# Block inversion on GpSimd, and the second memory scores inside the third query projection

## The chip, the core and the metric

The kernel runs on one core of one Trainium2 chip. The core has five engines with a queue of instructions each: TensorE (PE; matmuls, with PEld for its weight loads), VectorE (DVE), ScalarE (ACT), GpSimd (POOL) and SyncE (SP, which here only issues transfers). [...] Tiles live in SBUF (on-chip memory) and, for matmul results, in PSUM, whose banks GpSimd does not use in this kernel. Transfers between the device's memory and SBUF run on 16 engines of their own; those issued from SP are called hardware_dynamic in the profile, those from POOL software_dynamic. The metric is the device time of one execution in microseconds, as the median of several runs.

## The reference

Two layers over 512 tokens of width 1024. The change lies in the first, a gated DeltaNet layer with six heads of 128 and a cross-attention with four heads of 64 into 256 memory tokens. Cut to what matters:

```python
proj = h @ w_in                        # q, k, v (6 heads x 128 each), z, gates, mem_q (256)
qkv = silu(causal_depthwise_conv(proj[..., :o1], conv_w))
q, k = l2_normalize(q), l2_normalize(k)
# per chunk and head:
lower = where(strict, (k * beta) @ k.T * decay, 0)
sol = triangular_solve(lower, [v * beta, k * beta * exp(gc)], unit_diagonal=True)
u, w = sol
intra = (q @ k.T) * decay
# scan over the chunks of a head:
v_new = u - w @ state
o = (q * exp(gc)) @ state + intra @ v_new
state = state * g_last + k_g.T @ v_new
# beside it, per memory head:
p = softmax(mem_q @ mem_k.T / 8);  mem_o = p @ mem_v
# then: output projection, residual, SwiGLU; the second layer is sliding-window attention
```

## The kernel before

**Layout.** Activations are held transposed, 128 features by 512 tokens, as eight pairs (`self.h`) of a rounded high part and the remainder (`h`, `l` in the profile). The kernel uses chunks of 128 tokens, so NC = 4 chunks and NH = 24 head-chunks. A projection (`projected`, line 208) takes a weight tile of 128 by 1024 (`wraw`, two buffers, loaded from SP at line 177), splits it into `whi` on ScalarE (line 138) and `wlo` on VectorE (line 151), and runs eight steps of three matmuls (`mm3`, line 196; the profile shows them at line 144) into a bank of the tag `pj`. It is a generator: a caller can take a few steps, put other work in between, and go on.

**Banks.** In this stage PSUM has three banks `pj`, two `g`, three `sc` (line 255). Key products, query products and transposes go to `g`; memory scores take two of `g`, then two of `sc`.

**Order.** Instructions go to each engine's queue in an order that a planner fixes beforehand, from the program's order and modelled costs; a queue runs in that order. `nosync(ins, after)` (line 114) puts one instruction behind another in that order, without a semaphore wait. `self.last` is the last matmul of a step, `self.loaded` the last weight load issued from SP.

**The stage (`gdn`, line 552).** Keys are projected, normalized and turned; for each head-chunk the strict lower triangle goes to `N` (line 629). Its 32 by 32 diagonal blocks, four per head-chunk and 96 in all, are written to memory (`basein`, line 634). Then come the z projections with their Silu, and in between the first memory queries. At line 658 ScalarE's table is set to the exponentials and the first memory scores are made (`scores`, line 909: eight matmuls of a 64-row half each, maxima on VectorE, exponentials on ScalarE). After the second memory queries stands `base_inverse` (line 772):

- It loads the 96 blocks with one block on each partition (`L`, shown as `big`), clears `X` with ones on its diagonal, and inverts all blocks at once by 31 steps of two `tensor_tensor` on VectorE (lines 789 and 791; shown at line 151 as `btmp` and `big`), from 96x31 up to 96x256 elements and down again.
- ScalarE makes a turned copy (line 793). SP stores both (`basex`, `basext`, line 797) and loads them back as block diagonals: `X64` with four transfers (line 804, shown as `X`), `Tt` with four (line 809). VectorE clears both first; all clearings are held behind the last `N` (`known`).

**Queries and memory.** Two groups of three heads follow (line 698). `memory(m, first, late)` (line 667) makes the scores of memory half m (only for m = 1, with the table set to the exponentials again), projects the group's first query, takes two steps of the second, then the query products left in `late`, then `weigh` (line 959: scale the probabilities, transpose them into `g`, evict to `pf` on ScalarE, multiply by the values into `sc`), and the other six steps. The convolution (`conv_tile`, line 542) is one ScalarE copy and three VectorE instructions per head on `qv` (five buffers). Then the table goes to Silu and each head's `query` (line 683) runs: four products `g<-qv,kn`, `DT` and `gcr` multiplied on VectorE, a square `sq` (one buffer) on ScalarE, which SP stores. Of the first group, heads 0 and 1 run at once, behind the third projection; head 2 is put into `late` and runs in the second group's second projection. So the order on TensorE is: query projections 0, 1 (with the first weighing), 2, query products 0 and 1, second scores, projections 3, 4 (with query product 2 and the second weighing), 5.

**After it.** `solve` (line 812) extends the inverse from 32 to 64 and to 128 by products on TensorE. Its first products `sc<-X,N` need X64, the next ones Tt. Value projections and the scan follow. In the later stages GpSimd issues transfers that add to their target and does four multiplications near the end; in this stage it has nothing to do.

Of the kernel before, what the change touches and what calls it, by code (L numbers as in the profile page):

```python
# [18 lines left out]
P = 128  # L19
# [3 lines left out]
H = 6  # L23
# [61 lines left out]
class Builder:  # L85
# [466 lines left out]
    def gdn(self, gp):  # L552
# [67 lines left out]
        for h in range(H):  # L620
# [7 lines left out]
            for c in range(NC):  # L628
                known = self.stt(N[h][:, c, :], ps[:, chunk(c)], br[h][:, c:c + 1], d[:, c, :], ALU.mult, ALU.mult)
# [31 lines left out]
        X, every_t = self.base_inverse(gp, base_in, known)  # L661
        Tt = [every_t[:, h * NC:(h + 1) * NC, :] for h in range(H)]
# [4 lines left out]
        def memory(m, first, late):  # L667

            if m:
                self.use(LN_EXP)  # L670
                scores.append(self.scores(gp, qm[m], self.memK[m], False))
            ps = self.normed(first)
# [25 lines left out]
        for h0 in (0, 3):  # L698
            ps = memory(h0 // 3, h0, late)
            ts = [self.conv_tile(h0 + n, self.t(gp, [P, T], F32, "qv", 5), ps[n] if n < 2 else None) for n in range(3)]  # L700
            behind = self.last
            self.use(SILU_SIN)
            for h, t in zip(range(h0, h0 + 3), ts):
                self.fn(t, t, AF.Silu)
                if h == 2:
                    late.append((h, t))
                else:
                    query(h, t, behind)
# [63 lines left out]
    def base_inverse(self, gp, base_in, after):  # L772
# [10 lines left out]
        clear = lambda out, value: self.nosync(nc.vector.memset(out, value).ins, after)  # L783
        clear(Xf, 0.0)
        clear(Xf[:, ::BASE + 1], 1.0)
        for j in range(BASE - 1):
            r, w = BASE - 1 - j, j + 1
            tmp = self.t(gp, [n, 256], F32, "btmp", 2)[:, :r * w].rearrange("p (i m) -> p i m", m=w)
            self.tt(nc.vector, tmp, L[:, j, j + 1:].unsqueeze(2).to_broadcast([n, r, w]),
                    X[:, j, :w].unsqueeze(1).to_broadcast([n, r, w]), ALU.mult)  # L790
            self.tt(nc.vector, X[:, j + 1:, :w], X[:, j + 1:, :w], tmp, ALU.subtract)
        Xt = big(0)
        self.copy(Xt, X.rearrange("p i m -> p m i"))
        outs = []
        for nm, src in (("basex", X), ("basext", Xt)):
            d = self.t(self.dpool, [NH, NB, BASE * BASE], F32, nm)
            nc.sync.dma_start(d.rearrange("n b e -> (n b) e"), src.rearrange("p a b -> p (a b)"))
            outs.append(d)
        X64 = self.t(gp, [P, NH, 2 * BASE], F32, "X64")
        clear(X64, 0.0)  # L800
        for b in range(NB):
            s = slice(b * BASE, (b + 1) * BASE)
            o = b % 2 * BASE
            nc.sync.dma_start(X64[s, :, o:o + BASE], outs[0][:, b, :].rearrange("n (i m) -> i n m", m=BASE))
        Tt = self.t(gp, [P, NH, P], F32, "Tt")
        clear(Tt, 0.0)
        for b in range(NB):
            s = slice(b * BASE, (b + 1) * BASE)
            nc.sync.dma_start(Tt[s, :, s], outs[1][:, b, :].rearrange("n (m i) -> m n i", i=BASE))
# [99 lines left out]
    def scores(self, pool, q, kk, win, sinks=None):  # L909
# [8 lines left out]
        for n0 in range(0, NC, 2):  # L918
# [5 lines left out]
            for n in (n0, n0 + 1):  # L924
                ks = slice((n - 1) * P if n else 0, (n + 1) * P) if win else slice(0, ML)
                c0 = P if win and n == 0 else 0
                for b in range(2):
                    self.ahead = self.mm(ps[b][:, n - n0, c0:], q[half[b], n * P:(n + 1) * P], kk[half[b], ks])
                    if self.valued is not None:

                        self.nosync(self.ahead, self.valued)
                        self.valued = None
            for b in range(2):
# [805 lines left out]
```

## Time and profile before

| | us |
|---|---|
| three runs | 1116.19, 1117.37, 1118.53 (median 1117.37) |
| the profiled execution | 1116.54 |
| its span, first to last instruction | 1114.8 |
| TensorE busy | 1103.3 |
| VectorE busy | 936.2 |
| ScalarE busy | 696.7 |
| GpSimd busy | 105.9 |

The span is 1.7 us shorter than the profiled execution's time; the granted clock is 0.999. The page gives for each engine busy time, share of the span and instructions. Matmuls are pipelined, and one counts as busy from its start to a modelled end, so a full row of TensorE does not mean that it never waited; its weight loads (PEld) show waits better. "a <- b" in a group of waits says that a stood still until b ended. In a timeline a row gives start, length, engine, line, output and inputs, with the wait before it in brackets. The slices of the page show GpSimd nearly empty up to about 300 us of the span:

```
POOL 0000000000011111111110000000111111111101
```

### The profile page before, as it was taken

Reading aid. Unit: us, or ns where it says so; the run is one execution under the profiler, and the core shown is the slowest. Engines: PE = TensorE matmul, PEld = TensorE weight load, DVE = VectorE, ACT = ScalarE, POOL = GpSimd, SP = SyncE. Lnnn points to the kernel's source line nnn. Section 1 sums busy time; section 2 is a strip of 40 time slices with the busy share of each in tenths; the row PEclk is TensorE's granted clock in tenths of the full one; section 3 lists DMA queues with packets and bytes.
Section 4 is the critical chain, followed back from the end, with each engine's and each line's share of the span. In section 5 each row is a group of like instructions: output and inputs, shape, how many; then the busy total and the mean of one; then the engine's idle time right before and its main releaser. Section 6 shows DMA issues by size and latency. Waiting matters only on the chain.

```text
span 1114.8 us, 21268 instructions
## 1 busy us (share of the span) xinstructions
PE 1103.3 (99%) x7957; PEld 1000.3 (90%) x7957; DVE 936.2 (84%) x1886; ACT 696.7 (62%) x1466; POOL 105.9 (9%) x129
## 2 busy tenths in 40 slices
PE   9999999999999999999999999999999999999997
PEld 8888778877889999999998777788899999999996
DVE  7675977667899999999997877839999899998964
ACT  7588674466556656665565564866766566655644
POOL 0000000000011111111110000000111111111101
PEclk9999999999999999999999999999999999999999
DMA  8344352234467787778853321114678877777632
GB/s 319 99 153 145 107 142 87 86 100 137 148 165 196 186 193 190 178 184 197 199 138 99 118 72 39 57 58 142 161 174 196 198 180 182 191 192 198 154 85 90
DMA packets 81146, 165.36 MB, mean 148 GB/s; under 512 B 18588, under 2 KB 20148, under 8 KB 81044
## 3 DMA queue, kind: packets, MB, share of 16 engines
q1 hardware_dynamic: 64436, 133.87, 38.0%
q0 software_dynamic: 16320, 29.89, 16.4%
q8 instruction: 62, 1.02, 0.4%
q14 instruction: 40, 0.33, 0.1%
q10 hardware_dynamic: 288, 0.26, 0.1%
HBM read 156.98 MB, written 7.01 MB: 147 GB/s over the span
## 4 chain that ended last, share of the span: by engine, by line
PE 78%; DVE 17%; ACT 2%; issue 2%; DMA 0%; DVEq 0%; ACTq 0%; SPq 0%
PE g L144 43%; PE pj L144 23%; PE sc L144 6%; DVE wlo L151 5%; PE qk L144 2%; DVE fu L151 2%; PE pt L148 1%; DVE wraw L151 1%; PE pt L144 1%; DVE l L154 1%; DVE x L151 1%; DVE T L151 1%; DVE l L151 1%; DVE sqa L151 1%; DVE fg L151 1%
## 5 line engine op out<-in xcount | busy, mean ns | idle before, releaser
L138 ACT ACTIVATE whi<-wraw 128x512 fp32r<-128x512 f32 (+2 forms) x357 | 251.8, 711 | 156.5 <-PE g L144 68.6
L151 DVE TENSOR_TENSOR wlo<-wraw,whi 128x512 fp32r<-128x512 f32 (+2 forms) x357 | 279.3, 788 | 34.8 <-ACT whi L138 28.8
L144 PE MATMUL g<-T,whi 128*128 128x256 f32 x1280 | 228.8, 279 | 0.7 <-ACT fs L138 0.6
L144 PE MATMUL g<-l,whi 128*128 128x256 f32 (+1 forms) x780 | 222.9, 286 | 0.5 <-DVE l L151 0.5
L144 PE MATMUL g<-h,whi 128*128 128x256 f32 (+1 forms) x780 | 222.6, 285 | 0.0
L144 PE MATMUL g<-h,wlo 128*128 128x256 f32 (+1 forms) x780 | 222.5, 285 | 0.0
L144 PEld LDWEIGHTS g<-T,whi 128*128 128x128 f32 x1280 | 195.1, 188 | 1.6 <-ACT fs L138 1.1
L144 PE MATMUL pj<-h,whi 128*128 128x512 f32 (+1 forms) x460 | 182.1, 399 | 0.0
L144 PE MATMUL pj<-l,whi 128*128 128x512 f32 (+1 forms) x460 | 180.3, 392 | 0.6 <-DVE l L154 0.6
L144 PE MATMUL pj<-h,wlo 128*128 128x512 f32 (+1 forms) x460 | 179.8, 392 | 0.0
L144 PE MATMUL g<-T,wlo 128*128 128x256 f32 x640 | 178.5, 279 | 0.0
L144 PEld LDWEIGHTS g<-l,whi 128*128 128x128 f32 x780 | 146.6, 188 | 3.0 <-DVE l L151 1.1
L144 PEld LDWEIGHTS g<-h,whi 128*128 128x128 f32 x780 | 146.6, 188 | 1.9
L144 PEld LDWEIGHTS g<-h,wlo 128*128 128x128 f32 x780 | 146.6, 188 | 1.7
L144 PEld LDWEIGHTS g<-T,wlo 128*128 128x128 f32 x640 | 120.3, 188 | 0.0
L144 PEld LDWEIGHTS pj<-h,whi 128*128 128x128 f32 x460 | 86.3, 188 | 20.7 <-issue 4.1
L144 PEld LDWEIGHTS pj<-l,whi 128*128 128x128 f32 x460 | 86.6, 188 | 18.2 <-DVE l L154 1.7
L144 PEld LDWEIGHTS pj<-h,wlo 128*128 128x128 f32 x460 | 86.5, 188 | 17.9 <-issue 0.9
L138 ACT ACTIVATE whi<-ws 128x512 fp32r<-128x512 f32 x112 | 70.3, 627 | 44.5 <-PE g L144 42.0
L151 DVE TENSOR_TENSOR wlo<-ws,whi 128x512 fp32r<-128x512 f32 x112 | 76.5, 683 | 3.6 <-ACT whi L138 3.6
L1386 POOL DMA_DIRECT2D ws<-in_wgu x40 | 35.1, 878 | 447.7 <-DVE sqa L151 203.9
L138 ACT ACTIVATE fs<-g 128x256 f32<-128x256 f32 x168 | 61.5, 366 | 1.3 <-PE g L144 0.9
(398 smaller groups left out, 1926.5 us busy)
## 6 DMA issues: line engine op xcount, KB each, us to landing
wraw<-in_wgu SPq DMA_DIRECT2D x48, 512.0 KB
ws<-in_wgu SPq DMA_DIRECT2D x80, 256.0 KB
ws<-in_wgu POOLq DMA_DIRECT2D x80, 256.0 KB, 5.3
wraw<-in_win SPq DMA_DIRECT2D x26, 512.0 KB
wraw<-in_wgu SPq DMA_DIRECT2D x40, 256.0 KB
wraw<-in_wout SPq DMA_DIRECT2D x16, 512.0 KB
ws<-in_wdn SPq DMA_DIRECT2D x32, 256.0 KB
ws<-in_wdn POOLq DMA_DIRECT2D x32, 256.0 KB, 5.5
```

What stands on the lines that cost most here:

```text
L138: self.copied = self.nc.scalar.activation(out, in_, AF.Copy, **kw).ins
L144: return self.nc.tensor.matmul(out, lhsT, rhs, start=start, stop=stop, skip_group_check=more).ins
L148: return self.nc.tensor.transpose(out, in_, self.ident[:k, :k]).ins
L151: return eng.tensor_tensor(out=out, in0=a, in1=b, op=op).ins
L154: return self.nc.vector.scalar_tensor_tensor(out=out, in0=in0, scalar=scalar, in1=in1, op0=op0, op1=op1).ins
L1386: nc.gpsimd.dma_start(s1, a22, accum_op=ALU.add)
```

## The change

Four things are done.

1. The inversion's 62 `tensor_tensor`, the turned copy, the clearings of `X`, `X64` and `Tt` go to GpSimd. The two stores are issued from GpSimd's queue instead of SP's. The clearings are no longer held behind `N`.
2. The loads of `X64` and `Tt` stay on SP but are split off into `base_blocks`, called in the second group after `memory`, and held behind the last weight load issued there, that of the fifth query projection.
3. The second memory scores are made two steps into the third query projection, by a new argument `after` of `scores`; the table is not set to the exponentials again.
4. All three heads of the first group are put into `late`. The query products 0 and 1 run three steps into the fourth projection, product 2 two steps into the fifth as before.

```diff
--- before.py
+++ after.py
@@ -626,7 +626,7 @@
             for c in range(NC):
                 self.mm(ps[:, chunk(c)], kn[h][:, chunk(c)], kn[h][:, chunk(c)])
             for c in range(NC):
-                known = self.stt(N[h][:, c, :], ps[:, chunk(c)], br[h][:, c:c + 1], d[:, c, :], ALU.mult, ALU.mult)
+                self.stt(N[h][:, c, :], ps[:, chunk(c)], br[h][:, c:c + 1], d[:, c, :], ALU.mult, ALU.mult)
             if h % 2:
                 for b in range(NB):
                     s = slice(b * BASE, (b + 1) * BASE)
@@ -658,18 +658,19 @@
         self.use(LN_EXP)
         scores = [self.scores(gp, qm[0], self.memK[0], False)]
         memory_queries(1)
-        X, every_t = self.base_inverse(gp, base_in, known)
-        Tt = [every_t[:, h * NC:(h + 1) * NC, :] for h in range(H)]
+        outs = self.base_inverse(gp, base_in)
         for i in range(NH):
             h, c = divmod(i, NC)
             self.copy(kg[h][:, c, :], kg[h][:, c, :], scale=f[:, 2, i:i + 1])
 
         def memory(m, first, late):
 
+            steps = self.projected(a["win"][first], self.h)
             if m:
-                self.use(LN_EXP)
-                scores.append(self.scores(gp, qm[m], self.memK[m], False))
-            ps = self.normed(first)
+                nxt = [next(steps) for _ in range(3)]
+                while len(late) > 1:
+                    query(*late.pop(0), self.last)
+            ps = list(steps)[-1]
             steps = self.projected(a["win"][first + 1], self.h)
             nxt = [next(steps) for _ in range(2)]
             self.ahead = self.last
@@ -697,12 +698,22 @@
         late = []
         for h0 in (0, 3):
             ps = memory(h0 // 3, h0, late)
-            ts = [self.conv_tile(h0 + n, self.t(gp, [P, T], F32, "qv", 5), ps[n] if n < 2 else None) for n in range(3)]
+            if h0:
+                X, every_t = self.base_blocks(outs, self.loaded)
+                Tt = [every_t[:, h * NC:(h + 1) * NC, :] for h in range(H)]
+            conv = lambda n, ps: self.conv_tile(h0 + n, self.t(gp, [P, T], F32, "qv", 5), ps)
+            ts = [conv(n, ps[n]) for n in range(2)]
+            steps = self.projected(a["win"][h0 + 2], self.h)
+            if not h0:
+                for _ in range(2):
+                    next(steps)
+                scores.append(self.scores(gp, qm[1], self.memK[1], False, self.last))
+            ts.append(conv(2, list(steps)[-1]))
             behind = self.last
             self.use(SILU_SIN)
             for h, t in zip(range(h0, h0 + 3), ts):
                 self.fn(t, t, AF.Silu)
-                if h == 2:
+                if h < 3:
                     late.append((h, t))
                 else:
                     query(h, t, behind)
@@ -769,7 +780,7 @@
         finish(second)
         return mix + mq
 
-    def base_inverse(self, gp, base_in, after):
+    def base_inverse(self, gp, base_in):
 
         nc = self.nc
         n = NH * NB
@@ -780,33 +791,37 @@
         nc.sync.dma_start(L.rearrange("p a b -> p (a b)"), base_in.rearrange("n b e -> (n b) e"))
         X = big(1)
         Xf = X.rearrange("p a b -> p (a b)")
-        clear = lambda out, value: self.nosync(nc.vector.memset(out, value).ins, after)
-        clear(Xf, 0.0)
-        clear(Xf[:, ::BASE + 1], 1.0)
+        self.blocks = [self.t(gp, [P, NH, n], F32, nm) for nm, n in (("X64", 2 * BASE), ("Tt", P))]
+        for out, value in ((Xf, 0.0), (Xf[:, ::BASE + 1], 1.0), *((x, 0.0) for x in self.blocks)):
+            nc.gpsimd.memset(out, value)
         for j in range(BASE - 1):
             r, w = BASE - 1 - j, j + 1
             tmp = self.t(gp, [n, 256], F32, "btmp", 2)[:, :r * w].rearrange("p (i m) -> p i m", m=w)
-            self.tt(nc.vector, tmp, L[:, j, j + 1:].unsqueeze(2).to_broadcast([n, r, w]),
+            self.tt(nc.gpsimd, tmp, L[:, j, j + 1:].unsqueeze(2).to_broadcast([n, r, w]),
                     X[:, j, :w].unsqueeze(1).to_broadcast([n, r, w]), ALU.mult)
-            self.tt(nc.vector, X[:, j + 1:, :w], X[:, j + 1:, :w], tmp, ALU.subtract)
+            self.tt(nc.gpsimd, X[:, j + 1:, :w], X[:, j + 1:, :w], tmp, ALU.subtract)
         Xt = big(0)
-        self.copy(Xt, X.rearrange("p i m -> p m i"))
+        nc.gpsimd.tensor_copy(Xt, X.rearrange("p i m -> p m i"))
         outs = []
         for nm, src in (("basex", X), ("basext", Xt)):
             d = self.t(self.dpool, [NH, NB, BASE * BASE], F32, nm)
-            nc.sync.dma_start(d.rearrange("n b e -> (n b) e"), src.rearrange("p a b -> p (a b)"))
+            nc.gpsimd.dma_start(d.rearrange("n b e -> (n b) e"), src.rearrange("p a b -> p (a b)"))
             outs.append(d)
-        X64 = self.t(gp, [P, NH, 2 * BASE], F32, "X64")
-        clear(X64, 0.0)
+        return outs
+
+    def base_blocks(self, outs, after):
+
+        nc = self.nc
+        X64, Tt = self.blocks
         for b in range(NB):
             s = slice(b * BASE, (b + 1) * BASE)
             o = b % 2 * BASE
-            nc.sync.dma_start(X64[s, :, o:o + BASE], outs[0][:, b, :].rearrange("n (i m) -> i n m", m=BASE))
-        Tt = self.t(gp, [P, NH, P], F32, "Tt")
-        clear(Tt, 0.0)
+            self.nosync(nc.sync.dma_start(
+                X64[s, :, o:o + BASE], outs[0][:, b, :].rearrange("n (i m) -> i n m", m=BASE)).ins, after)
         for b in range(NB):
             s = slice(b * BASE, (b + 1) * BASE)
-            nc.sync.dma_start(Tt[s, :, s], outs[1][:, b, :].rearrange("n (m i) -> m n i", i=BASE))
+            self.nosync(nc.sync.dma_start(
+                Tt[s, :, s], outs[1][:, b, :].rearrange("n (m i) -> m n i", i=BASE)).ins, after)
         return X64, Tt
 
     def solve(self, gp, N, X64, Tt):
@@ -906,7 +921,7 @@
         return new
 
 
-    def scores(self, pool, q, kk, win, sinks=None):
+    def scores(self, pool, q, kk, win, sinks=None, after=None):
 
         nc = self.nc
         own = "pt" in self.pbufs
@@ -930,6 +945,9 @@
 
                         self.nosync(self.ahead, self.valued)
                         self.valued = None
+                    if after is not None:
+                        self.nosync(self.ahead, after)
+                        after = None
             for b in range(2):
                 i = b * NC + n0
                 if win:
```

## What the change does to the time: the prediction

> **What bounds the kernel now.** First the page: busy time of each engine, then the chain of work that ended last.
>
> ```profile
> PE 1103.3 (99%) x7957; PEld 1000.3 (90%) x7957; DVE 936.2 (84%) x1886; ACT 696.7 (62%) x1466; POOL 105.9 (9%) x129
> ...
> PE 78%; DVE 17%; ACT 2%; issue 2%; DMA 0%; DVEq 0%; ACTq 0%; SPq 0%
> ```
>
> TensorE is never out of work for long. The change lies between 100 and 180 us of the span. There the chain in order of time (start, length) runs mostly through VectorE, from its first row to its last one here:
>
> ```profile
> 118.36 1.23 DVE wlo L151
> ...
> 148.30 0.61 DVE DT L151
> ```
>
> But TensorE beside it is just as full. What can be won is not VectorE's time itself, only the moments at which TensorE stood still. The waits of its weight loads from 106 to 176 us (total, times, longest) give the upper limit:
>
> ```profile
> PEld pj L144 <- issue: 1.4, 4, 0.4
> PEld sc L144 <- ACT pf L138: 1.3, 4, 0.4
> PEld g L144 <- DVE DT L151: 1.0, 2, 0.8
> PEld g L148 <- issue: 0.8, 2, 0.4
> PEld g L144 <- issue: 0.4, 1, 0.4
> PEld g L148 <- ACT pf L138: 0.3, 1, 0.3
> PEld g L144 <- ACT qv L132: 0.2, 1, 0.2
> ```
>
> Together 5.4 us. No edit here can win more than that, 0.5% of the span. The place where the wait for DT stands, below the first block of scores, in the timeline of TensorE (start, length):
>
> ```profile
> 117.07 0.39 PE L144 MATMUL pj<-h,wlo 128*128 128x512 f32 x1
> 117.39 1.13 PE L144 MATMUL g<-m,qm 64*128 64x256 f32 x8
> ...
> 119.31 0.50 PE L144 MATMUL pj<-h,whi 128*128 128x512 f32 x1
> ...
> 145.22 0.39 PE L144 MATMUL pj<-l,whi 128*128 128x512 f32 x1
> 145.44 0.40 PE L144 MATMUL pj<-h,wlo 128*128 128x512 f32 x1
> 145.68 2.22 PE L144 MATMUL g<-qv,kn 128*128 128x128 f32 x16
> ...
> 148.95 1.13 PE L144 MATMUL g<-m,qm 64*128 64x256 f32 x4 [0.42 <-DVE DT L151]
> ...
> 151.80 0.50 PE L144 MATMUL pj<-h,whi 128*128 128x512 f32 x1
> ```
>
> A projection starts a matmul every 0.23 us (145.22, 145.44), so its 24 take 5.45 us and a step of three 0.68. The first scores take 2.01 us between two projections (117.07 + 0.23 to 119.31). The second scores stand behind two query products, and both together take 6.13 us (145.44 + 0.23 to 151.80): the scores want the g banks, which VectorE empties (DT) only after other queued work.
>
> **The change, part by part.**
>
> *Second scores into the third projection.* No matmul is added or removed. The third projection ends at 145.67, so it starts at 140.2, and the scores now begin two steps into it, at 141.6 us, long after the first weighing has left the g banks. I charge them like the first ones, 2.01 us. The two query products go three steps into the fourth projection. What one such product of eight records costs inside a projection, in the timeline of the weight loads:
>
> ```profile
> 158.50 1.09 PEld L144 LDWEIGHTS g<-qv,kn 128*128 128x128 f32 x8
> 159.51 0.47 PEld L148 LDWEIGHTS g<-consts,sm 128*128 128x128 f32 x4
> ```
>
> It is 1.01 us to the next load, twice that 2.0 us. Gain: 6.13 − 2.01 − 2.0 = 2.1 us. Two of ScalarE's table loads disappear too, since no return to the exponential table lies between the scores and the Silus. One of them stands right ahead of the second weighing's first eviction:
>
> ```profile
> 124.47 0.24 ACT L132 ACTIVATION_READ_ACCUMULATOR sm<-sc,nm 128x1 f32 x1
> ...
> 159.40 1.28 ACT L123 ACT_TABLE_LOAD   x1
> 160.69 0.60 ACT L138 ACTIVATE pf<-g 128x512 f32<-128x512 f32 x1
> 161.19 1.05 ACT L138 ACTIVATE whi<-wraw 128x1024 fp32r<-128x1024 f32 x1
> ```
>
> TensorE waits for pf 1.6 us in all over both weighings (1.3 and 0.3); I count 0.4 us as won, between nothing and 0.8 (one weighing of two). Sum of this part: 2.5 us.
>
> *Inversion to GpSimd.* What VectorE spends on it from 111 to 150 us, what shares VectorE with it, and the rows of GpSimd that come nearest (busy us, mean ns, idle before):
>
> ```profile
> L151 DVE TENSOR_TENSOR big<-big,btmp 96x31 f32<-96x31 f32 (+15 forms) x31 | 10.4, 337 | 0.7
> L151 DVE TENSOR_TENSOR btmp<-big 96x31 f32<-96x31 f32 (+15 forms) x31 | 10.4, 334 | 2.6 <-DMA big<-basein 1.9
> L151 DVE TENSOR_TENSOR wlo<-wraw,whi 128x1024 fp32r<-128x1024 f32 x5 | 6.1, 1216 | 0.2 <-ACT whi L138 0.2
> ...
> L151 DVE TENSOR_TENSOR gcr<-gcr,qv 128x512 f32<-128x512 f32 x2 | 1.4, 692 | 0.1
> L994 DVE TENSOR_SCALAR sm<-sm,den 128x256 f32<-128x256 f32 x4 | 1.4, 345 | 0.0
> ...
> L151 DVE TENSOR_TENSOR btmp<-big 96x256 f32<-96x256 f32 x1 | 0.4, 421 | 0.0
> ...
> L151 POOL TENSOR_TENSOR T<-T,ws 128x256 f32<-128x256 f32 x4 | 2.8, 731 | 57.5 <-ACT ws L132 57.5
> ...
> L1498 POOL MEMSET cosT<- 128x512 f32 x1 | 0.5, 527 | 42.4 <-DVE gcr L154 42.4
> ```
>
> VectorE loses 20.8 us in 62 instructions, each dependent on the last, on either engine. At 256 columns GpSimd takes 731 ns against 421, a factor of 1.74: 20.8 × 1.74 = 36 us. From both sides: 20.8 us if GpSimd were as quick, 62 × 0.731 = 45 us if short rows cost as much as 256 columns. I take 36, and 2 us for spacing. The loop begins when its input lands (the wait of 1.9 us, which ended at 111.3), so it ends near 149.3. The turned copy of 1024 columns costs between 1.05 us (two of the 512-column clearing) and 2.9 (four of 731 ns); I take 2.9: 152.2. The clearings come before the input, when GpSimd is empty: nothing.
>
> *Stores and loads.* SyncE's queue before, the first uses on TensorE, the transfers that GpSimd issued (median to landing), and one row of the busy time by windows (the last but one column is the share of the transfer engines):
>
> ```profile
> 143.44 0.33 SPq L177 DMA_DIRECT2D wraw<-in_win  x1
> ...
> 149.02 0.33 SPq L797 DMA_DIRECT2D basex<-big  x1
> ...
> 152.02 2.33 SPq L804 DMA_DIRECT2D X<-basex  x4
> ```
>
> ```profile
> 175.22 1.71 PE L144 MATMUL sc<-X,N 32*32 32x32 f32 x96
> ...
> 180.92 0.21 PE L144 MATMUL sc<-Tt,big 32*32 32x32 f32 x1
> ```
>
> ```profile
> ws<-in_wgu POOLq DMA_DIRECT2D x80, 256.0 KB, 5.3
> ```
>
> ```profile
> 160.00:162.00 2.00, 2.00 (x16) 1.74 (x14) 1.97 (x4) 1.99 (x3) 0.00 (x0) 1.00 0.28 102
> ```
>
> From SyncE the store took 3.0 us to the load that waits for it (149.02 to 152.02). From GpSimd I take 5.3 us, the landing of its larger transfers: the loads may start at 157.5. Before, the eight loads had left the transfer engines by about 160 (share down to 0.28), 8 us after the first issue, so the X half, issued first, in about 4. X64 stands at 161.5 and Tt at 165.5. They are used at 175.22 and 180.92, by the gain 2.5 us earlier: 172.7 and 178.4. Spare: 11 us for X64, 13 for Tt. So the inversion costs nothing; what hides it is the query projections four to six, and without them each microsecond would be a microsecond of TensorE. What is freed on VectorE wins nothing beyond the waits counted above.
>
> **Sum.** The profiled execution took 1116.5 us: 1116.5 − 2.5 = 1114.0. The median of the three runs, 1117.4, lies 0.9 above it, so I expect a median of 1114.9. The forecast's own range is 1113.2 (the whole 1.6 us for pf goes, and half a microsecond of issue) to 1116.4 (1.0 us won).
>
> **Rivals.**
>
> 1. *The queries wait for their Silu instead (no change).* The first three Silus now stand behind the second exponentials and a table load. The first scores needed from 117.39 to 124.7 until the last exponential; from 141.6 that gives 148.9, plus 1.3 for the table and 1.3 for two Silus at a 512-column pass of 0.6: 151.5. The products are allowed from 149.7 (145.67 + 2.01 + three steps). TensorE can do further steps first, if the order lets it. If not, it loses 1.8 us: 1115.8, as a median 1116.7. Against it: the first scores' reductions had a wlo of 1.2 us ahead of them on VectorE, which is emptier now.
>
> 2. *GpSimd is late (slower).* Place: the first products of the solve. If short instructions cost like long ones (45 us) and GpSimd also waits out the VectorE rows above that read two tiles or scale sm (6.1 + 1.4 + 1.4 = 8.9), the loop takes 18 us more than 36. With 11 us spare TensorE stands for 7 us: 1114.0 + 7 = 1121.0, as a median 1121.9. It decides from a loop that ends past 160.5. For it: nothing before shows a dependent chain on GpSimd. [...] Against it: the sum above has slow choices already.
>
> 3. *SyncE's queue stands still (slower).* The block loads are ordered only behind the load of the fifth query weights. If they also come ahead of the sixth weights' load (143.44 before), this one waits behind all eight, to 165.5, and 2 us more, and then for its split, 1.05 us on ScalarE and 1.2 on VectorE: 169.8. The sixth projection starts no later than 175.22 − 2.0 (two products) − 5.45 = 167.8, by the gain at 165.3: 4.5 us late, 1118.5, as a median 1119.4. Behind the same head wait the stores of the squares, whose one buffer ScalarE needs next. Against it: before, the same loads stood behind 143.44.
>
> **How the numbers follow.** Chances: forecast 0.54, rival 1 0.18, rival 2 0.15, rival 3 0.13. About 0.2%, 2.2 us, is what a measurement tells from no change; the forecast's 2.5 us is just above, so 0.37 of its 0.54 is faster and 0.17 the same. With rival 1 (0.03 faster, 0.15 the same) and mild forms of the others (0.02 the same): faster 0.40, same 0.34, slower 0.26. The range goes from 1113.2 to 1122.0, the price of rival 2.
>
> **What would show it.** Right: the second scores stand at 141 to 144 us without a wait for DT; btmp and big stand on GpSimd and end before 160; the X loads are issued before 168; the first product on X comes at about 172.7. Wrong: a weight load of TensorE waiting for X or Tt (rival 2), for whi or wlo at the sixth projection (rival 3), or for ACT qv at the query products (rival 1). [...] A step of the sum fails if GpSimd's mean lies outside 0.34 to 0.73 us.

## The result, and the profile after

| | before | after |
|---|---|---|
| median (runs) | 1117.95 us (4) | 1130.32 us (4; 1129.47 to 1131.84) |
| profiled execution, its span | 1116.54, 1114.8 | 1131.84, 1130.0 |
| granted clock | 0.999 | 0.994 |

The changed kernel is slower: the ratio is 1.0114, with a 95% interval of 1.0099 to 1.0130. The forecast was 1114.9, its range ended at 1122.0.

The page of the changed kernel, busy time of each engine and the chain that ended last:

```profile
PE 1106.6 (98%) x7957; PEld 1003.6 (89%) x7957; DVE 922.1 (82%) x1820; ACT 692.9 (61%) x1463; POOL 149.1 (13%) x198
...
PE 76%; DVE 14%; POOL 3%; issue 2%; ACT 2%; DMA 2%; SPq 0%; DVEq 0%; ACTq 0%; POOLq 0%
```

VectorE lost 14.1 us of busy time and GpSimd got 43.2. What left VectorE were 25.7 us (the inversion's 20.8 and 4.9 of clearings), so the rest of its rows grew by 11.6; examples stand further down (`negc`, `gcr`). POOL and DMA now have a share of the chain (3% and 2%; before, DMA had 0% and POOL none): something of the inversion or its transfers came to stand on the path. The waits of TensorE's weight loads from 145 to 200 us say where (total, times, longest):

```profile
PEld g L144 <- ACT qv L132: 12.5, 2, 10.5
```

Before, no entry of this window was above 1.0 us. TensorE's timeline of the changed kernel has both waits in brackets, and between them a projection at its normal pace:

```profile
142.65 1.13 PE L144 MATMUL g<-m,qm 64*128 64x256 f32 x8
...
148.83 0.39 PE L144 MATMUL pj<-h,whi 128*128 128x512 f32 x1
...
153.30 2.05 PE L144 MATMUL g<-qv,kn 128*128 128x128 f32 x16 [1.59 <-ACT qv L132]
...
159.06 0.39 PE L144 MATMUL pj<-h,wlo 128*128 128x512 f32 x1
169.55 2.07 PE L144 MATMUL g<-qv,kn 128*128 128x128 f32 x8 [10.10 <-ACT qv L132]
...
172.70 0.63 PE L144 MATMUL pj<-l,whi 128*128 128x512 f32 x1
173.13 0.63 PE L144 MATMUL pj<-h,wlo 128*128 128x512 f32 x1
...
188.39 1.71 PE L144 MATMUL sc<-X,N 32*32 32x32 f32 x96
```

The first products on X stand at 188.39 us, 13.2 later than before (175.22). These rows make up the sum. The second scores begin at 142.65 in place of the forecast 141.6, because the changed kernel is already 1.0 us late there, 0.8 of it by the clearings (below). The fourth projection begins at 148.83, 3.0 us *earlier* than before (151.80): the scores without a wait for DT won 4.0. Of that, 2.0 are two query products that now come later (153.30: the edit allows them from the third step of the fourth projection on, and they came after its fourth). Then come 1.6 us of waiting for Silu, 10.1 us for another Silu, and a stretch at half speed: from 169.55 to 174.1 us (the end follows from the clock windows in the last section) a projection starts a matmul every 0.43 us (172.70, 173.13), not every 0.23, which costs half of 4.6, 2.3 us. 1.0 − 4.0 + 2.0 + 1.6 + 10.1 + 2.3 = 13.0, so 0.2 us stay unexplained. Behind the solve the profiled execution slowly loses 2 us more; it was the longest of four, and two others took 2.3 us less.

Why did a Silu take so long? ScalarE's queue, SyncE's queue, and the wait of SyncE's own queue (from 100 to 200 us), all of the changed kernel:

```profile
167.92 1.06 ACT L138 ACTIVATE whi<-wraw 128x1024 fp32r<-128x1024 f32 x1 [12.04 <-DMA wraw<-in_win]
168.89 0.61 ACT L132 ACTIVATE qv<-qv 128x512 f32<-128x512 f32 x1
```

```profile
120.75 10.14 SPq L177 DMA_DIRECT2D wraw<-in_win  x2
158.56 2.11 SPq L819 DMA_DIRECT2D X<-basex  x4
160.76 2.34 SPq L823 DMA_DIRECT2D Tt<-basext  x4
163.20 0.95 SPq L177 DMA_DIRECT2D wraw<-in_win  x2
164.24 6.68 SPq L696 DMA_DIRECT2D q<-sq  x2
```

```profile
SPq L819 <- DMA basex<-big: 27.6, 1, 27.6
```

Read from the bottom: SyncE stood for 27.6 us on the first block load, which waits for GpSimd's store. Right behind it waited the sixth query weights and the stores of the squares. The load of the weights was issued at 163.2 and landed just before their split `whi` (167.92), and this split stands in ScalarE's queue *ahead of the third Silu* (168.89), and the third query product needs that Silu. Nobody needed those weights yet: the fifth projection had only taken its second step. A wait at the head of one queue reached TensorE through the head of another.

### The profile page after: what moved, and what is told of

Read it like the earlier page. It is cut to its first block, busy times and chain, and to the rows that moved or that the text cites. A ratio compares the mean times of both kernels' runs of the same rounds, so it can differ in the third digit from the quotient of the medians.

```text
span 1130.0 us, 21273 instructions
## 1 busy us (share of the span) xinstructions
PE 1106.6 (98%) x7957; PEld 1003.6 (89%) x7957; DVE 922.1 (82%) x1820; ACT 692.9 (61%) x1463; POOL 149.1 (13%) x198
## 4 chain that ended last, share of the span: by engine, by line
PE 76%; DVE 14%; POOL 3%; issue 2%; ACT 2%; DMA 2%; SPq 0%; DVEq 0%; ACTq 0%; POOLq 0%
PE g L144 44%; PE pj L144 21%; PE sc L144 5%; DVE wlo L151 4%; PE qk L144 3%; POOL big L151 2%; DVE fu L151 2%; POOL btmp L151 2%; PE pt L144 1%; PE pt L148 1%; DVE wraw L151 1%; DVE x L151 1%; DVE l L154 1%; DVE T L151 1%; PE g L148 1%
```

## The experiments

"Median" is that of a kernel's own runs; a ratio is to the kernel before on the same chip, with its 95% interval.

### Which part loses: each alone

**The scores part alone**: the inversion stays on VectorE as before; scores and queries are moved.

```diff
-        outs = self.base_inverse(gp, base_in)
+        X, every_t = self.base_inverse(gp, base_in, known)   # as before, VectorE
```

> Only the scores and query products are moved; the inversion stays on VectorE, the stores and block loads on SyncE as before. By my sum 2.1 us are won; if the first query products wait for their Silu as they did in the changed kernel (1.7 us), 0.4 us. So 1115.8 to 1117.6 by that theory, ratio 0.998 to 0.9997. If the moved scores were themselves the cause of the long wait, 1125 or more.

**The inversion part alone**: scores and queries stand as before; GpSimd's inversion and the ordered block loads are kept.

```diff
-                nxt = [next(steps) for _ in range(3)]
-                while len(late) > 1:
-                    query(*late.pop(0), self.last)
+                self.use(LN_EXP)
+                scores.append(self.scores(gp, qm[m], self.memK[m], False))
```

> Only the inversion, the copy, the clearings and the stores go to GpSimd and the block loads behind the fifth query weights; scores and query products stay as before. Theory A: the sixth weights' load stands behind the block loads, ScalarE stands at its split, and TensorE waits some 10 us and then runs at the slow clock: 1126 to 1132. If the wait needs both parts (the query products behind the split), the sixth projection alone waits, 4 to 6 us: 1122 to 1125. Rival B as before: a wait at the first product on X.

Measured: scores alone 1120.53 us, ratio 1.0025 [1.0016, 1.0034]; inversion alone 1137.00, 1.0176 [1.0162, 1.0190]. Both lose, and the inversion alone loses more than the two together. Both miss what was expected: the scores alone were to be no slower than before, and the inversion alone was to lose less, through the sixth weights' split. ScalarE's timeline and then TensorE's, first with the inversion alone, then with the scores alone:

```profile
162.93 0.63 ACT L692 ACTIVATE sq<-qv 128x512 f32<-128x512 f32 x1 [17.07 <-DMA q<-sq]
```

```profile
165.57 2.47 PE L144 MATMUL g<-m,qm 64*128 64x256 f32 x6 [17.07 <-DVE DT L151]
```

```profile
146.59 0.47 ACT L132 ACTIVATE sm<-g,nm 128x256 f32<-128x256 f32 x1 [4.93 <-DVE nm L158]
...
148.76 2.11 ACT L138 ACTIVATE big<-big 96x1024 f32<-96x1024 f32 x1 [0.24 <-issue]
...
154.57 1.15 ACT L132 ACTIVATE qv<-qv 128x512 f32<-128x512 f32 x2
```

```profile
155.26 3.78 PE L144 MATMUL g<-qv,kn 128*128 128x128 f32 x16 [2.88 <-ACT qv L132]
```

In the first, the first square's store hangs behind the first block loads, the second square waits 17 us for the one buffer, the copy of the third query stands behind that square on ScalarE, its taps stand ahead of DT on VectorE, and the old place of the scores needs the banks that DT empties. In the second, ScalarE waits 4.9 us for the maxima before its first exponential, later its own turned copy takes 2.1 us, and the Silus start only at 154.57: the query products wait 2.9 us and then run at half speed (16 in 3.78 us against 2.05).

### Whose queue the loads stand in

**Block loads on GpSimd's queue**, behind its own stores:

```diff
-            self.nosync(nc.sync.dma_start(X64[...], ...).ins, after)
+            nc.gpsimd.dma_start(X64[...], ...)          # and the same for Tt
```

> The changed kernel, but the eight block loads are issued from GpSimd's own queue, behind its stores, so that nothing on SyncE's queue stands behind them. Theory A (the loss is SyncE's queue standing behind the block loads, with GpSimd itself in time): the 10 us wait of the query products and the slow clock after it are gone; what is left is the clearings (+0.8 us), the moved scores (-2.1) and the first query's wait for its Silu (+1.7), so 1116.5 to 1118.5 us, ratio to before 0.999 to 1.001. Rival B (GpSimd delivers too late for the solve): TensorE then waits at the first product on X, and the time stays above 1125. Rival C (GpSimd beside VectorE slows the splits): wlo stays long and the time stays above 1122.

**Block loads on SyncE, behind the sixth weights' load:**

```diff
-            if h0:
-                X, every_t = self.base_blocks(outs, self.loaded)
...
+            else:
+                first = next(steps)       # the third projection of the group: its load is issued
+                X, every_t = self.base_blocks(outs, self.loaded)
```

> The changed kernel, but the block loads are held behind the load of the sixth query weights instead of the fifth. If that one weight load is all that the queue delays (my third rival as I wrote it), the time is 1116.5 to 1118.5. If everything behind the queue's head counts, the next victim is the store of the first square: ScalarE's second square needs its buffer, stands until the block loads are out (near 165 us) and holds what is behind it on ScalarE; TensorE then waits 3 to 8 us at the second weighing's evictions: 1120 to 1126. Rival B (GpSimd too late): 1125 and more, with the wait at the first product on X.

Measured: on GpSimd's queue 1121.99, ratio 1.0040 [1.0027, 1.0052], with nothing left of the 10 us. Of the 4 us beyond the expectation the trace has 2.1 as a wait of TensorE for the eviction `pf`, which stands on ScalarE behind a square that waits for its one buffer, and 1.7 as a stretch of 3.4 us at half clock after it. The splits `wlo` were a little longer (1302 ns on average from 100 to 170 us, 1212 before), but TensorE waited for none of them, so rival C is not what held it. Behind the sixth weights 1129.21, 1.0107 [1.0093, 1.0121], above both ranges that were expected: the weights are in time now, and the wait is as long as before, at the next thing behind the same head. ScalarE's and TensorE's timelines of this second kernel:

```profile
166.44 0.63 ACT L694 ACTIVATE sq<-qv 128x512 f32<-128x512 f32 x1 [9.94 <-DMA q<-sq]
```

```profile
170.39 1.97 PE L148 MATMUL g<-consts,sm 128*128 128x128 f32 x8 [9.51 <-ACT pf L138]
```

The second square waits for the store of the first, which waits behind the block loads; the weighing's eviction `pf` waits behind that square.

**Two buffers for the squares, nothing else** (only the chain's second link is taken away):

```diff
-            sq = self.t(gp, [P, T], F32, "sq", 1)
+            sq = self.t(gp, [P, T], F32, "sq", 2)
```

> The changed kernel with two buffers for the squares and nothing else. Theory (the ten microseconds come from the sixth weights, whose load waits behind the block loads and whose split stands ahead of the third Silu on ScalarE): the wait of the query product stays near 10 us, time 1128-1131. Rival (the chain goes through the squares' one buffer): the wait falls below 4 us, 1119-1123.

**Loads behind the second square's store**, one buffer:

```diff
-            nc.sync.dma_start(q2[h], sq)
+            self.stored = nc.sync.dma_start(q2[h], sq).ins
+            self.stores = getattr(self, "stores", []) + [self.stored]
...
-                X, every_t = self.base_blocks(outs, self.loaded)
+                X, every_t = self.base_blocks(outs, self.stores[1])   # placed as above, after the sixth load
```

> Only the place of the eight block loads in SyncE's queue is changed: behind the load of the sixth query weights and the second square's store, nothing else. Theory (SyncE's head is what cost the ten microseconds): no wait of TensorE above 4 us is left between 140 and 180 us, the time falls from 1130.3 to 1119-1123 (like the kernel with the loads on GpSimd's queue, 1122.0). Rival (the loads themselves or their traffic cost it, wherever they stand): it stays above 1127.

**Both:**

> Like the kernel before in this list, and the squares have two buffers in place of one. Theory (the second square waits for the store of the first, and the weighing's eviction pf stands behind it on ScalarE: 2.25 us at 161-164 us with the loads on GpSimd's queue): the wait of ACT sq for the store goes, and 1.5 to 3 us with it, 1117.5-1120.5. Rival (pf is late for another reason, the exponentials): the wait of pf stays and so does the time, within 1 us of the kernel with one buffer.

**The inversion part alone, with both:**

> The inversion part alone (second scores and queries as in the kernel before), with the block loads behind the second square's store on SyncE and two buffers for the squares. Theory (GpSimd's work itself is hidden, only the place of the loads in the queue cost 19 us): 1116-1119, no wait of TensorE above 2 us from 140 to 185 us. Rival (VectorE, slowed by GpSimd beside it, is late for the second scores): the wait for DT stays above 3 us and is followed by a half clock, above 1120.

| kernel | median us | ratio, 95% interval |
|---|---|---|
| two buffers alone | 1131.85 | 1.0145 [1.0117, 1.0173] |
| loads behind the second store | 1120.73 | 1.0035 [1.0022, 1.0048] |
| both | 1116.22 | 0.9996 [0.9986, 1.0006] |
| inversion alone, with both | 1116.72 | 0.9992 [0.9983, 1.0002] |

Two buffers alone win nothing. The wait only moves: ScalarE's and then TensorE's timeline of that kernel show `whi` behind the same head, now with `pf` behind it:

```profile
167.30 1.06 ACT L138 ACTIVATE whi<-wraw 128x1024 fp32r<-128x1024 f32 x1 [12.06 <-DMA wraw<-in_win]
```

```profile
172.22 1.12 PE L148 MATMUL g<-consts,sm 128*128 128x128 f32 x4 [12.18 <-ACT pf L138]
```

With the loads moved and one buffer, ScalarE and then TensorE show what is left of the second link: the third square waits until the second one's store has landed.

```profile
162.18 0.63 ACT L694 ACTIVATE sq<-qv 128x512 f32<-128x512 f32 x1 [2.53 <-DMA q<-sq]
```

```profile
163.34 1.09 PE L148 MATMUL g<-consts,sm 128*128 128x128 f32 x8 [2.54 <-ACT pf L138]
```

With both, that wait and the one for the weights are gone; what TensorE's weight loads still wait for `pf` at line 148, from 100 to 200 us (3.3 with one buffer), is this:

```profile
PEld g L148 <- ACT pf L138: 0.5, 2, 0.3
```

The ratio to the kernel before falls from 1.0114 to 0.9996, some 13 us, by two edits that don't touch a computation. In the last kernel GpSimd's inversion costs nothing that can be measured against the kernel before. So the loss was the place of the block loads in a queue (some 9 us: 1.0114 to 1.0035) and the squares' one buffer (the other 4), not GpSimd's speed.

### The clearings

**The kernel with loads on GpSimd's queue, and the clearings on VectorE** behind the last product of N:

```diff
-            nc.gpsimd.memset(out, value)
+            self.nosync(nc.vector.memset(out, value).ins, known)
```

> The kernel with the block loads on GpSimd's queue (1122.0), with the four clearings back on VectorE behind the last product of N. Theory (a VectorE row waits out GpSimd's clearings at 54 us, and that cost 0.8 us): the 4.11 us row of negc goes back to about 0.18, the start of the first scores comes 0.8 us earlier, 1120.7-1121.5. Rival (VectorE pays for the clearings where it does them, about 5 us of its time between 105 and 112 us, and TensorE waits for them there): same or slower, 1122 or more.

VectorE's timelines: of the changed kernel, with GpSimd's clearings beside it (below), and of this one.

```profile
54.49 4.11 DVE L158 TENSOR_SCALAR negc<-negc 128x24 f32<-128x24 f32 x1 [0.26 <-ACT negc L132]
```

```profile
53.62 0.95 POOL L796 MEMSET big<- 96x1024 f32 x1 [13.29 <-PE g L144]
...
55.90 2.66 POOL L796 MEMSET Tt<- 128x3072 f32 x1
```

```profile
54.01 0.18 DVE L158 TENSOR_SCALAR negc<-negc 128x24 f32<-128x24 f32 x1 [0.26 <-ACT negc L132]
```

A row of 0.18 us took 4.11 and ended with the last clearing (55.90 + 2.66 = 58.56). The key taps came later and TensorE waited 0.7 us for them. With the clearings on VectorE the row and the wait are as before. The time, 1121.42, ratio 1.0041 [1.0025, 1.0057], can't be told from that of the same kernel with GpSimd's clearings (1.0040): the lengthening of the row is shown, its price not beyond the profile. In the kernel with both mends above, GpSimd's first clearing happened to come 6 us earlier, and the row took 0.55.

### What became of the moved scores' gain

In the kernels so far that have moved scores and GpSimd's inversion, the two query products wait 1.4 to 1.6 us for Silu. Seven kernels look for what holds it. The first takes all mends together and allows the products later:

```diff
-                nxt = [next(steps) for _ in range(3)]
+                nxt = [next(steps) for _ in range(7)]     # beside loads, two buffers, clearings on VectorE
```

> All mends together: block loads behind the second square's store on SyncE, two buffers for the squares, clearings on VectorE, and the two query products not before the seventh step of the fourth projection in place of the third. Theory (the moved scores win 2 us, and the rest of the loss is head of SyncE's queue, buffer, clearings and the wait for Silu): no wait above 1 us is left between 140 and 180 us, 1114.5-1117. Rival (Silu is late whatever stands ahead of it, since the second exponentials end at about 150 us): a wait of 1 to 2 us for ACT qv stays, with a stretch of half clock behind it, 1117.5-1120.

The second puts the scores at the very start of the third projection (loads behind the second store and two buffers in this and in all that follow, but for the last, whose loads stay where they were before):

```diff
-                for _ in range(2):
-                    next(steps)
                 scores.append(self.scores(gp, qm[1], self.memK[1], False, self.last))
```

> The kernel with loads behind the second square's store and two square buffers (1116.2), with the second scores at the very start of the third projection, not two steps into it. Theory (the query products wait 1.5 us for Silu because the exponentials begin late): scores, exponentials and Silus come 1.0 to 1.4 us earlier, the wait falls to 0.1-0.6 us, 1115.0-1115.8. Rival (the reductions on VectorE stand behind the split and taps, which don't move): the exponentials come at most 0.3 us earlier and the time stays at 1116-1117.

The third, beside that, puts two Silus ahead of the third query's copy on ScalarE:

```diff
-            ts.append(conv(2, list(steps)[-1]))
+            last = list(steps)[-1]
...
+                if n == 2:                                # in the loop of the Silus
+                    ts.append(conv(2, last))
```

> The same, with the first two Silus ahead of the third query's copy on ScalarE. Theory: the Silus come 0.6 us earlier still, the wait for them vanishes, 1114.5-1115.5. Rival (the third Silu, now behind its own later copy and taps and a weight split, is what the third product waits for): a new wait of 0.5 us or more at the third product, 1116 or more.

Measured: 1117.54, ratio 1.0004 [0.9994, 1.0013]; 1117.64, 1.0001 [0.9992, 1.0011]; 1117.23, 0.9998 [0.9988, 1.0007]. None of the three comes into its range. In the first, the two products no longer wait, but three waits of about 0.5 us stand behind them (for the third Silu, `pf` and DT). In the other two they still wait 1.7 and 1.5 us, as the second's rival had it. VectorE and ScalarE of the second kernel, with the scores at the start of the projection, show why:

```profile
140.66 1.61 DVE L151 TENSOR_TENSOR wlo<-wraw,whi 128x1024 fp32r<-128x1024 f32 x1 [2.70 <-ACT whi L138]
142.19 0.74 DVE L154 SCALAR_TENSOR_TENSOR qv<-pj,gains,qv 128x511 f32<-128x511 f32 x1
142.85 0.68 DVE L963 TENSOR_REDUCE mx<-g 128x2 f32<-128x512 f32 x1
143.45 0.73 DVE L154 SCALAR_TENSOR_TENSOR qv<-pj,gains,qv 128x510 f32<-128x510 f32 x1
```

```profile
144.35 0.47 ACT L132 ACTIVATE sm<-g,nm 128x256 f32<-128x256 f32 x1 [3.15 <-DVE nm L158]
```

The scores were there by 141.6, but the first maximum stands behind the split of the fifth weights and a tap, the next behind another tap. The exponentials began at 144.35; with the scores 1.4 us later they had begun at 144.59. So the next kernel orders VectorE: the four reductions first, then taps and split.

```diff
+            w = self.weight(a["win"][first + 1])
+            if m:
+                self.nosync(self.low, self.negated)      # the split's low part behind the last nm
...
-            ts = [conv(n, ps[n]) for n in range(2)]
+            ts = [conv(0, ps[0])]                        # conv 1 after the scores, its first tap
+                self.nosync(self.tap0, self.negated)     # behind the last nm
```

> Scores at the start of the third projection, loads behind the second square's store, two square buffers (1117.6), and on VectorE the four reductions of the second scores stand ahead of the second query's taps and of the fifth weights' split. Theory (VectorE's order holds the exponentials): they begin about 2 us earlier, at 142 us, no wait for Silu is left at the query products, and the time falls by 1.5 to 2 us to 1115.6-1116.2. Rival (ScalarE's own length holds them): the wait stays above 1 us, 1117 or more.

The same with GpSimd's turned copy in four parts; then that with the scores two steps in again; then the scores part alone with VectorE ordered so:

```diff
+        for i in range(0, BASE, 8):
+            nc.gpsimd.tensor_copy(Xt[:, i:i + 8], X.rearrange("p i m -> p m i")[:, i:i + 8])
```

> The same, with GpSimd's turned copy in four parts of 256 columns. Theory (a VectorE row of two tiles waits out the whole copy of 2.0 us, and DT and the weighing come late behind it): the row of gcr falls from about 2.5 to 1.3 us or less, and with it 0.3 to 0.7 us of TensorE's waits, 1115.0-1115.8. Rival (nothing on TensorE hangs on it): the same time within 0.3 us as the kernel with one copy.

> As the last one, but the second scores two steps into the third projection, as in the changed kernel. Theory (only VectorE's order mattered): within 0.5 us of the kernel with the scores at the start. Rival (each step later is a step of waiting for Silu): a wait of 0.7 to 1.4 us, slower by as much.

> The scores part alone (inversion on VectorE, its turned copy on ScalarE as before), with the scores at the start of the projection, the reductions ahead of taps and split, and two square buffers. Theory (the part is worth its 2 us once the exponentials come early): 1115.0-1116.2, against 1120.5 for the part alone as it was made. Rival (the inversion on VectorE or its copy on ScalarE holds the Silus in any case, and only with GpSimd's help can the scores be moved): a wait above 1 us and a half clock stay, 1118 or more.

| kernel | median us | ratio, 95% interval |
|---|---|---|
| reductions first | 1116.28 | 0.9988 [0.9978, 0.9997] |
| and the copy in four parts | 1116.02 | 0.9987 [0.9978, 0.9996] |
| and the scores two steps in | 1116.78 | 0.9988 [0.9979, 0.9998] |
| scores alone, reductions first | 1116.47 | 0.9991 [0.9982, 1.0001] |

With the reductions first, VectorE and ScalarE show:

```profile
140.84 1.29 DVE L972 TENSOR_REDUCE mx<-g 128x2 f32<-128x512 f32 x2 [2.90 <-PE g L144]
```

```profile
142.30 0.47 ACT L132 ACTIVATE sm<-g,nm 128x256 f32<-128x256 f32 x1 [1.11 <-DVE nm L973]
...
147.37 1.16 ACT L132 ACTIVATE qv<-qv 128x512 f32<-128x512 f32 x2
```

The exponentials come 2.05 us earlier, the Silus 3.7 (147.37 against 151.11; 0.6 of this because the third query's copy now stands behind them), and no wait for Silu is left. This version beats the kernel before by 0.12% [0.03, 0.22]: small, and only just clear of the interval. It was not run on one chip with the kernels of the old order, whose best ratio was 0.9996 [0.9986, 1.0006]. The copy in four parts took no measurable time off; the four parts together took 4.0 us, the one copy 2.1. With the scores two steps in, 0.77 us of waiting came back, and the time moved by no more than can be measured. With the scores alone, ScalarE's own turned copy stands between table and Silus and keeps 1.24 us of waiting; its time can't be told from the kernel before, and the loss that it had (1.0025) is gone. The rows of these two kernels, TensorE's for the first, ScalarE's and TensorE's for the second:

```profile
150.55 2.05 PE L144 MATMUL g<-qv,kn 128*128 128x128 f32 x16 [0.77 <-ACT qv L132]
```

```profile
148.91 2.07 ACT L138 ACTIVATE big<-big 96x1024 f32<-96x1024 f32 x1
```

```profile
151.55 2.05 PE L144 MATMUL g<-qv,kn 128*128 128x128 f32 x16 [1.24 <-ACT qv L132]
```

One thing stays open. In all kernels with moved scores, except the changed one and the one with two buffers alone, TensorE's order is another one as far away as 296 us, and TensorE waits 1.3 us there for a residual sum on VectorE. In the kernel with both mends the lead over the kernel before is 0.9 us at 290 us and 0.2 at 326. Holding that order fixed was not tried.

## Why the prediction was wrong, point by point

**The cost of the block loads' place** failed, and it alone is larger than the range. The forecast said "So the inversion costs nothing; what hides it is the query projections four to six", and rival 3 saw the queue come to stand, priced at 4.5 us with a chance of 0.13. The place was right, and so, nearly, was the time of the weights (165.5 and 2 more; their split began at 167.92). The price followed one thing behind the head, the sixth weights, down to its own first use on TensorE at 165 us. It should have asked who stands *behind the split of these weights* on ScalarE: the third Silu, wanted at 159. The rival's sentence "Behind the same head wait the stores of the squares, whose one buffer ScalarE needs next" named the other link and gave it no time. In its place stands a wait of TensorE of 10.1 us for that Silu, inside the fifth projection and not at the sixth. The runs show that each link alone brings a wait of that size (9.5 us through the square, 12.2 through the weights), and that their prices are not added.

**The half clock** was no term at all. After the wait of 10 us it cost 2.3.

**Second scores: 6.13 − 2.01 − 2.0 = 2.1 us.** Right as a term: they stand without a wait for DT, and the fourth projection begins 4.0 us early of which 2.0 are the products. What failed was its neighbour, rival 1 with its chance of 0.18: the wait for Silu was there in the changed kernel (1.6 us; priced at 1.8). The forecast argued against it that VectorE "is emptier now". It is, but a queue's order is no matter of how full it is: the reductions still stood behind a split and two taps.

**0.4 us from pf** didn't come, though the table load ahead of it is gone. The two weighings still cost 1.7 us of TensorE's waits with both mends (1.6 before).

**GpSimd's loop** was right in its size, in part by luck. The groups of GpSimd from 100 to 160 us and the ends of its work:

```profile
L151 POOL TENSOR_TENSOR big<-big,btmp 96x31 f32<-96x31 f32 (+15 forms) x31 | 19.3, 623 | 2.4
L151 POOL TENSOR_TENSOR btmp<-big 96x31 f32<-96x31 f32 (+15 forms) x31 | 16.9, 545 | 56.1 <-DMA big<-basein 53.8
```

```profile
153.09 0.25 POOL L151 TENSOR_TENSOR big<-big,btmp 96x31 f32<-96x31 f32 x1
153.40 2.00 POOL L804 COPY big<-big 96x1024 f32<-96x1024 f32 x1
155.36 0.54 POOL L808 DMA_DIRECT2D basex<-big  x1
```

36.2 us busy against 36. But five of the 62 rows stood beside a split `wlo` on VectorE and took some 0.9 us longer each (one is shown in the last section), about 4.3 us together. Without that the loop had taken some 32 us, a factor of 1.5 to VectorE's 20.8 and not 1.74: the scaling was too high, and the rows beside VectorE made up for it. Rival 2 gave these 8.9 us, the whole length of eleven rows of VectorE; that was my assumption, and no run shows the term. In its place stand the 4.3 us beside the five splits; beside the four rows of `sm` (151.00, 1.47 us together) GpSimd's two rows of 87 columns took 0.40 and 0.34 us, against 0.33 and 0.36 on its way up (113.75, 114.15). The loop ended 4 us later than forecast (153.3 against 149.3), one for the later start, the rest nearly all for spacing: 31 pairs of rows with 4.8 us between them, not 2. The copy took 2.0 (2.9 forecast), the store 3.2 to the first load at 158.56 (5.3 forecast). So the loads were issued 1 us later than forecast and far inside the spare time, and no weight load of TensorE waited for these loads, nor did one in the kernel with both mends, where the products on X come at 174.28. As a whole rival 2 fell.

**Clearings "nothing"** was wrong by 0.8 us in the profile of this kernel: I looked for who waits for GpSimd, and not for whose rows get longer beside it. The splits `wlo` got longer in this kernel too: 1309 ns on average from 100 to 170 us, against 1212 before.

## What to carry to other kernels

When an instruction that will wait long is put into a queue, write down everything behind it in that queue, and for each of those everything behind *its* consumer on the consumer's engine, until TensorE; the first to be missed sets the price, and mending one link only shows the next. A load that waits for another engine's result belongs behind all loads and stores that are ready earlier, or on that engine's own queue. And a result moved earlier is worth nothing until its consumers' order on the next engine is moved too.

## What the runs showed of the hardware

**Half the clock after a short stop.** Windows of the changed kernel (length, then busy time and count by engine, granted clock, share of the transfer engines, GB/s):

```profile
160.00:165.00 5.00, 0.00 (x0) 0.00 (x0) 0.00 (x0) 0.00 (x0) 0.00 (x0) 0.89 1.09 173
165.00:170.00 5.00, 0.45 (x2) 0.45 (x3) 0.47 (x1) 1.64 (x3) 0.00 (x0) 0.50 0.71 239
170.00:175.00 5.00, 5.00 (x24) 4.49 (x24) 4.86 (x7) 3.28 (x6) 0.00 (x0) 0.59 0.53 178
```

A clock of 0.89, 0.50 and 0.59 in three windows of 5 us is half speed for (0.22 + 1.00 + 0.82) × 5 = 10.2 us: in windows of 1 us from 150 to 180 us it reads 1.00 or 0.50, but for the first and the last of the stretch (0.95 from 163 us, 0.93 from 174 us). With the scores alone a wait of 2.9 us was followed by some 6.9 us at half speed by the same reckoning (0.96, 0.50, 0.85), and with the loads on GpSimd's queue one of 2.1 us by 3.4 (0.66 in one window); with the clearings on VectorE besides, eight products `sc<-pf,m` behind a wait of 2.9 us took 1.98 us, and the next eight 1.08. But the wait of 2.5 us in the kernel with loads behind the second store and one buffer had none (1.00 from 160 to 175 us), nor had the waits of 1.4 to 1.6 us for Silu in the four kernels whose clock there was read (1.00). So waits of 2.1, 2.9 and 10.1 us cost more than themselves here, and one of 2.5 us did not. What decides it, no run shows.

**VectorE and GpSimd hold each other up, both ways.** Rows of the changed kernel: GpSimd's beside a split on VectorE, and the next of its kind without one; the split; VectorE's beside GpSimd's copy (153.40, above) and without it:

```profile
132.62 1.48 POOL L151 TENSOR_TENSOR btmp<-big 96x256 f32<-96x256 f32 x1
134.99 0.63 POOL L151 TENSOR_TENSOR btmp<-big 96x255 f32<-96x255 f32 x1
```

```profile
132.40 1.23 DVE L151 TENSOR_TENSOR wlo<-wraw,whi 128x1024 fp32r<-128x1024 f32 x1 [1.86 <-ACT whi L138]
```

```profile
153.43 2.53 DVE L151 TENSOR_TENSOR gcr<-gcr,qv 128x512 f32<-128x512 f32 x1
158.39 0.68 DVE L151 TENSOR_TENSOR gcr<-gcr,qv 128x512 f32<-128x512 f32 x1
```

GpSimd's row of 256 columns took 1.48 us beside the split, the one of 255 columns 0.63 without one. The split took 1.23 us, and 1.22 at 99.61 us, where GpSimd did nothing. The `gcr` row took 2.53 us beside GpSimd's copy of 2.00 and 0.68 without it. The row of `negc` above took 4.11 us beside three clearings in a row and 0.18 with the clearings on VectorE. Which of the two engines stands still, and for how long, no run shows beyond these rows.
